# Single slices and an earlier spread in the first modulation, and scaled values made ahead of the delta rule's solves

## The chip, the cores and the metric

The kernel runs on one core of a Trainium2 chip. The metric is the device time of one execution in microseconds (us). The work is done by TensorE (matrix products, PE in the profile, its weight loads PEld), VectorE (DVE), ScalarE (ACT) and GpSimd (POOL). SyncE (SP) issues the loads and stores.

## What is computed

One block of a streaming encoder over 512 tokens of width 1024: a feed-forward half step, a token mixer of two head groups (gated delta rule and latent attention), and a second half step. Each of the three begins with an RMS norm that is modulated by a scale and a shift, which a product of the vector `silu(c)` with a large matrix gives.

```python
sc = jax.nn.silu(c)
mod = sc @ w_ada[l] + b_ada[l]
sh1, s1, g1, sh2, s2, g2, sh3, s3, g3 = jnp.split(mod, N_MOD, axis=-1)
h = _modulate(x, sh1, s1)              # rms(x) * (1 + s1) + sh1
x = x + 0.5 * g1 * _swiglu(h, ffn1_w_in[l], ffn1_w_out[l])
...
h = _modulate(x, sh2, s2)
x = x + g2 * _hybrid_mixer(h, ...)
```

The delta rule works in chunks. In each chunk a unit lower triangular system is solved:

```python
M = A + jnp.eye(CHUNK)
rhs = concatenate([v * beta, k * (beta * exp(G))], axis=-1)
W = triangular_solve(M, rhs)
u, wk = W[..., :GDN_DV], W[..., GDN_DV:]
```

`u` and `wk` then enter a recurrence over the chunks that carries the state.

## The kernel before

Tokens lie along the free dimension, features on the 128 partitions: `xT` is eight tiles of 128 x 512. Every weight and every activation that enters a large product is split into a high part (a copy by ScalarE to fp32r) and a low part (a subtraction by VectorE), and a product is three matmuls: high by high, high by low, low by high (`mm3`, L453 to L455).

A framework turns the program into queues. It places each instruction on its engine by the order of the program and by times that it estimates, gives each tile a buffer of its pool, and puts in the waits. Within `in_order()` every engine keeps the written order. Outside, instructions may move ahead of each other where their inputs allow it. Engines issue strictly in their final order. PSUM has eight banks: three in the pool `psa` (`acc()`, tiles pa) and five in `psb` (`aux()`, tiles pb). The pool `slots` holds 56 tiles of 128 x 512 floats.

**The first modulation** is `phase0`, written inside `in_order()`. It makes the transposed input, the first shift and scale, the modulated input `h` and at the same time the first three column groups of the feed-forward input product, six accumulators `pu`. The loop over `kt` walks the eight row blocks of the contraction. For each it needs a slice of `w_ada` (1024 rows by twice 128 columns, 1024 KB), a slab of 768 columns of `ffn1_w_in` (384 KB), and `h[kt]`.

A slice comes in one of two ways. `phase0_slice` loads one alone with two loads into a buffer of the pool `p0`, which has two buffers. `phase0_pair` loads two neighbours with eight loads into eight slots. Slices 0 and 1 are single, 2 and 3, 4 and 5, 6 and 7 are pairs. `phase0_weights(kt)` loads a slab into one of four buffers `wr`; the slab of step kt + 2 is asked for in step kt. The loads are on SyncE's queue in the written order.

From a slice come two columns, shift and scale. For slices 0 to 4 and 6 `phase0_cols` does it with sixteen small matmuls (L632), ScalarE copies the sums (L635), and `columns` adds four partial rows with matmuls (L525) and the bias with two VectorE instructions (L526, L527). Slices 5 and 7 (`SUMMED`) are instead summed up by `phase0_sum`, one ScalarE step (L641) and seven VectorE steps (L643) each, spread over the steps 2 to 5 of the loop by the table `STEPS`.

`raw(b, j)` transposes half of a token block with four TensorE transposes (L507) and copies the result to `xT` by VectorE (L508). There are eight such tiles: seven stand ahead of the first columns, the eighth behind them. The norm's factors `r` are computed per token. For block 0 the tokens are scaled (`xn`) before they are transposed (L547). VectorE copies this to SBUF (L549), ScalarE makes the high part with scale and shift (L552), VectorE the whole value (L553) and the low part (L554), and then the low weights (L556). Then come the six first products (L569). Behind them a product of ones with a diagonal matrix spreads `r` over all partitions (`spread_diag`, L663), and ScalarE copies it to `rb` (L571). All later blocks use `rb` in `modulated` (L688, L690, L677).

**The mixer** runs its dense units, 128 output columns each, on TensorE in program order, and steps side chains between them. `Rates` gives each chain so many steps for each step of the dense unit. `chain` carries the decay, the inverses of the blocks (`base_blocks`, `inverse`) and then the solves. `deltas` carries `delta_qk` and `delta_q`. `att` carries the attention. The units come in the order keys, queries, values, gates. In the gate units the rates are 1, 0.75 and 2.67.

`solve(p)` turns the values of block p to token-major order with four transposes (L1489, from `token_major`), scales them by VectorE into `vb` (L1269, from `mul`, line of a helper), scales the keys into `kbg` and `kd` in the same way, then multiplies with the inverse `U`: L1689 for `uu`, L1698 for `w`. `recur(p)` is the recurrence. The output products of the attention half (`out_attended`, update of `xT` at L2119) are stepped in as filling work, and the first weights of the last feed-forward part are split on the side (L1264, L1265).

Of the kernel before, what the change touches and what calls it, by code (L numbers as in the profile page):

```python
# [28 lines left out]
KPARTS = ((0, 8), (8, 8), (16, 6))  # L29
SEVEN = range(8, 21), range(4, 21)  # L30
SUMMED = (5, 7)
STEPS = {2: (5, range(4)), 3: (5, range(4, 8)), 4: (7, range(4)), 5: (7, range(4, 8))}


def drain(*gens):

    gens = list(gens)
    while gens:
        for g in list(gens):
            if next(g, "end") == "end":  # L40
                gens.remove(g)
# [51 lines left out]
class Block:  # L93
# [390 lines left out]
    def phase0(self):  # L484

        nc = self.nc
        xall = self.const([P, KT, NT], s="xT")
        self.xT = [xall[:, t, :] for t in range(KT)]
        v = self.small(NB, "v")
        slices, parts = [], []  # L490
        for kt in range(2):
            slices.append(self.phase0_slice(kt))
            parts.append(self.phase0_weights(kt))
        slices += self.phase0_pair(2)
        pv = self.aux()
        nc.tensor.transpose(pv[:, :80], self.vecs[:80, :], self.ident[:80, :80])
        self.sc = self.const([P, 8], s="sc")
        nc.scalar.activation(self.sc, pv[:, 72:80], AF.Silu)
        self.vT = self.const([P, 72], s="vT")
        nc.vector.tensor_copy(self.vT, pv[:, :72])  # L500
# [3 lines left out]
        def raw(b, j):  # L504
            pt = self.aux()
            for t in range(4):
                nc.tensor.transpose(pt[:, t * P:(t + 1) * P], self.xtok[b][:, (4 * j + t) * P:(4 * j + t + 1) * P], self.ident)  # L507
            nc.vector.tensor_copy(xall[:, 4 * j:4 * j + 4, b * P:(b + 1) * P], pt.rearrange("p (t c) -> p t c", t=4))  # L508

        tiles = [(b, j) for b in range(NB) for j in range(2)]  # L510
# [8 lines left out]
        self.c1, self.c2 = self.const([P, KT], s="sh"), self.const([P, KT], s="s1")  # L519
        self.new_h()  # L520

        def columns(kt, sg, pg, ones):
            k = slice(kt, kt + 1)
            for m in range(2):
                nc.tensor.matmul(pg[:, 256 + m:257 + m], sg[:, m * P:m * P + P], ones, start=True, stop=True)  # L525
            nc.vector.tensor_tensor(out=self.c1[:, k], in0=pg[:, 256:257], in1=self.vT[:, k], op=ALU.add)  # L526
            nc.vector.scalar_tensor_tensor(out=self.c2[:, k], in0=pg[:, 257:258], scalar=1.0, in1=self.vT[:, 8 + kt:9 + kt],  # L527
                                           op0=ALU.add, op1=ALU.add)

        def weights(kt):  # L530
            raw, hi, lo = parts[kt]
            self.split_w(raw[:, :6, :], hi[:, :6, :], lo[:, :6, :])
            return hi, lo
# [8 lines left out]
        raw0, wh, wl = (x[:, :6, :] for x in parts[0])  # L542
        w = wh, wl
        nc.scalar.copy(wh, raw0)
# [4 lines left out]
        nc.vector.tensor_copy(t, pt)  # L549
        columns(0, *cols)  # L550
        hh, hl = self.h[0]
        nc.scalar.activation(hh, t, AF.Identity, scale=self.c2[:, 0:1], bias=self.c1[:, 0:1])  # L552
        nc.vector.tensor_scalar(out=m, in0=t, scalar1=self.c2[:, 0:1], scalar2=self.c1[:, 0:1], op0=ALU.mult, op1=ALU.add)  # L553
        nc.vector.tensor_tensor(out=hl, in0=m, in1=hh.bitcast(F32), op=ALU.subtract)  # L554
        self.kept[0] = m, None
        nc.vector.tensor_tensor(out=wl, in0=raw0, in1=wh.bitcast(F32), op=ALU.subtract)  # L556
        raw(*tiles[7])
        pu = [self.acc() for _ in range(3)] + [self.aux() for _ in range(3)]
        sums = {}
        for kt in range(KT):  # L560
            (hi, lo), (xh, xl) = w, self.h[kt]
            more = kt + 1 < KT
            if kt + 2 < KT:
                parts.append(self.phase0_weights(kt + 2))
            if kt in (1, 3):
                slices += self.phase0_pair(kt + 3)
            if kt == 0:
                for j in range(6):
                    nc.tensor.matmul(pu[j], hi[:, j, :], xh, start=True, stop=False)  # L569
                rb = self.slot(s="rb")  # L570
                nc.scalar.copy(rb, self.spread_diag(dg, NB))  # L571
            for j in range(6):
                if j == 0 and more:
                    if kt > 2:
# [5 lines left out]
                    if kt in (1, 2):  # L580
                        w = weights(kt + 1)
                if j == (2 if kt + 1 in SUMMED else 1) and more:
                    columns(kt + 1, *cols)
                    made = self.modulated([kt + 1], slice(0, NT), rb, self.c2, self.c1, True)
                    next(made)
                    n, kcs = STEPS.get(kt, (None, ()))
                    for i, kc in enumerate(kcs):
                        if kt == 2 or i == 2:
                            drain(made)
                        if kc == 0:  # L590
                            sums[n] = self.slot(s="sg")[:, :256]
                        self.phase0_sum(sums[n], slices[n], kc)
                    drain(made)
                    if kt == 0:
                        w = weights(kt + 1)
                if kt > 0:
                    self.mm3(pu[j], hi[:, j, :], lo[:, j, :], xh, xl, False, kt == KT - 1)
                else:
                    nc.tensor.matmul(pu[j], hi[:, j, :], xl, start=False, stop=False)
                    nc.tensor.matmul(pu[j], lo[:, j, :], xh, start=False, stop=False)  # L600
        return pu
# [797 lines left out]
    def gates(self):  # L1399
# [9 lines left out]
        v.tensor_tensor(out=t4(x), in0=kv[:, :, 64:68], in1=self.dtb.unsqueeze(1).to_broadcast([P, NB, 4]), op=ALU.add)  # L1409
# [260 lines left out]
    def solve(self, p, vT):  # L1670
# [297 lines left out]
    def mixer(self, norms):  # L1968
# [21 lines left out]
                self.table(t, t, AF.Silu, after=after)  # L1990

        self.inv = [None] * NB
        self.kd, self.us, self.o, self.wk = ([None] * NB for _ in range(4))
        self.S = None

        def prepared():
# [208 lines left out]
```

## Time and profile before

| | us |
|---|---|
| median of 3 runs | 1041.88 (1041.50 to 1042.18) |
| the profiled execution | 1041.97 |
| its span | 1040.3 |

The span runs from the first to the last instruction that the profiler saw; the execution's time has 1.67 us more around it. In the lists of the profile a row is: start, duration, engine, line, operation, output and inputs with their shapes, count, and in brackets the idle time of the engine ahead of it with what ended it. Matmuls are pipelined, so the rows of TensorE overlap. The granted clock of TensorE was 1.000 over the whole span.

### The profile page before, as it was taken

To read this page: it belongs to the slowest core of one execution; us is meant where nothing else is said; L and a number is where in the kernel's file an instruction comes from. 1 tells how busy PE (TensorE), PEld (TensorE's weight loads), DVE (VectorE), ACT (ScalarE), POOL (GpSimd) and SP (SyncE) were. 2 spreads that over 40 slices of the span, in tenths; PEclk is the share of its full clock that TensorE was granted. 3 is DMA by queue.
4 is the path that set the end of the run, shared out by engine and by line. 5 is a ranking of instruction groups with operands and counts; after the bars stand their busy time and mean duration, and the time that the engine had idled before them with its cause. 6 is when DMAs were issued, how large, how long until landed. Compare 5 with 4: busy or idle time off the path is not lost.

```text
span 1040.3 us, 16767 instructions
## 1 busy us (share of the span) xinstructions
PE 1023.9 (98%) x6601; PEld 907.6 (87%) x6601; DVE 753.8 (72%) x1327; ACT 498.5 (48%) x910; POOL 29.6 (3%) x74
## 2 busy tenths in 40 slices
PE   7999999999999999999999989999999999999998
PEld 5788899999887898888788779998999999987888
DVE  5789788887787757868697467787788888783221
ACT  4452455556322235478864454364555555632221
POOL 0000000001000000000000001100000000000000
PEclk9999999999999999999999999999999999999999
DMA  9977234334688744211232031103333334383311
GB/s 330 320 230 255 76 89 122 89 116 130 213 297 280 241 126 130 61 42 41 61 83 65 21 87 36 42 24 96 105 92 112 108 97 121 114 271 105 112 48 42
DMA packets 201501, 130.77 MB, mean 126 GB/s; under 512 B 14017, under 2 KB 186062, under 8 KB 201422
## 3 DMA queue, kind: packets, MB, share of 16 engines
q1 hardware_dynamic: 201422, 129.69, 40.7%
q8 instruction: 52, 0.85, 0.3%
q14 instruction: 27, 0.22, 0.1%
HBM read 127.18 MB, written 2.49 MB: 125 GB/s over the span
## 4 chain that ended last, share of the span: by engine, by line
PE 93%; DVE 3%; issue 1%; DMA 1%; POOL 0%; SPq 0%; ACT 0%; POOLq 0%
PE pa L453 17%; PE pa L454 17%; PE pa L455 17%; PE pa L341 17%; PE pb L341 12%; PE pb L1937 1%; PE pb L453 1%; PE pb L455 1%; PE pb L454 1%; PE pb L1917 1%; DMA ar<-in_w_ada 1%; PE pb L1537 1%; PE pb L632 1%; PE pb L1919 0%; PE pb L1489 0%
## 5 line engine op out<-in xcount | busy, mean ns | idle before, releaser
L223 ACT CAST wh<-wr 128x1024 fp32r<-128x1024 f32 (+1 forms) x104 | 103.6, 1002 | 198.7 <-PE pa L454 174.8
L224 DVE TENSOR_TENSOR wl<-wr,wh 128x1024 fp32r<-128x1024 f32 (+1 forms) x104 | 120.5, 1163 | 80.6 <-ACT wh L223 78.6
L453 PE MATMUL pa<-ah,wh 128*128 128x512 f32 (+1 forms) x396 | 146.5, 370 | 0.0
L454 PE MATMUL pa<-al,wh 128*128 128x512 f32 (+1 forms) x396 | 145.0, 366 | 0.0
L455 PE MATMUL pa<-ah,wl 128*128 128x512 f32 (+1 forms) x396 | 144.9, 366 | 0.0
L257 DVE TENSOR_TENSOR wl<-wr,wh 128x1024 fp32r<-128x1024 f32 x90 | 110.0, 1223 | 44.4 <-ACT wh L261 44.4
L453 PE MATMUL pa<-hh,wh 128*128 128x512 f32 (+1 forms) x357 | 136.9, 384 | 0.0
L454 PE MATMUL pa<-hl,wh 128*128 128x512 f32 (+1 forms) x357 | 135.2, 379 | 0.0
L455 PE MATMUL pa<-hh,wl 128*128 128x512 f32 (+1 forms) x357 | 135.2, 379 | 0.0
L261 ACT CAST wh<-wr 128x1024 fp32r<-128x1024 f32 x90 | 91.8, 1052 | 2.7 <-DMA ar<-in_w_ada 1.8
L453 PEld LDWEIGHTS pa<-ah,wh 128*128 128x128 f32 x396 | 74.7, 189 | 14.5 <-ACT wh L223 2.5
L455 PEld LDWEIGHTS pa<-ah,wl 128*128 128x128 f32 x396 | 74.7, 189 | 12.1
L454 PEld LDWEIGHTS pa<-al,wh 128*128 128x128 f32 x396 | 74.7, 189 | 11.7
L453 PEld LDWEIGHTS pa<-hh,wh 128*128 128x128 f32 x357 | 67.3, 189 | 13.3 <-ACT th L1264 0.8
L813 DVE SCALAR_TENSOR_TENSOR aa<-ar,sc,aa 128x512 f32<-128x512 f32 x98 | 73.3, 749 | 6.3 <-DMA ar<-in_w_ada 4.3
L455 PEld LDWEIGHTS pa<-hh,wl 128*128 128x128 f32 x357 | 67.3, 188 | 11.6
L454 PEld LDWEIGHTS pa<-hl,wh 128*128 128x128 f32 x357 | 67.4, 189 | 10.7
L341 PE MATMUL pa<-hh,wh 128*128 128x256 f32 x240 | 68.0, 283 | 0.0
L341 PE MATMUL pa<-th,wh 128*128 128x256 f32 x240 | 67.9, 283 | 0.0
L341 PE MATMUL pa<-tl,wh 128*128 128x256 f32 x240 | 67.9, 283 | 0.0
L341 PE MATMUL pa<-th,wl 128*128 128x256 f32 x240 | 67.9, 283 | 0.0
L341 PE MATMUL pa<-hl,wh 128*128 128x256 f32 x240 | 67.9, 283 | 0.0
(434 smaller groups left out, 2375.3 us busy)
## 6 DMA issues: line engine op xcount, KB each, us to landing
wr<-in_ffn_w_in SPq DMA_DIRECT2D x79, 512.0 KB, 5.0
ar<-in_w_ada SPq DMA_DIRECT2D x104, 256.0 KB, 5.6
wr<-in_ffn_w_out SPq DMA_DIRECT2D x32, 512.0 KB, 4.2
wr<-in_w_in SPq DMA_DIRECT2D x21, 512.0 KB, 4.3
ar<-in_w_ada SPq DMA_DIRECT2D x20, 512.0 KB, 5.9
wr<-in_ffn_w_out SPq DMA_DIRECT2D x16, 384.0 KB, 4.7
wr<-in_w_out SPq DMA_DIRECT2D x8, 512.0 KB, 3.3
wr<-in_ffn_w_in SPq DMA_DIRECT2D x8, 384.0 KB, 5.9
```

The lines of the kernel that those rows point to most:

```text
L223: self.nc.scalar.copy(hi, raw)
L224: self.nc.vector.tensor_tensor(out=lo, in0=raw, in1=hi.bitcast(F32), op=ALU.subtract)
L257: sub = lambda out, x, y: nc.vector.tensor_tensor(out=out, in0=x, in1=y, op=ALU.subtract)
L261: nc.scalar.copy(hi[:, :n], raw[:, :n])
L341: nc.tensor.matmul(z, a[:, j, :], b, start=start and j == 0 and i == 0, stop=j == 3 and i == 2, skip_group_check=not start)
L453: mm(out, wh, xh, start=start, stop=False)
L454: mm(out, wh, xl, start=False, stop=False)
L455: mm(out, wl, xh, start=False, stop=stop)
L632: nc.tensor.matmul(pg[32 * q:32 * q + 32, :256], self.sc[:, kc:kc + 1].to_broadcast([P, 32]), a[kc], start=(e == 0), stop=(e == 1), tile_p ...
L813: nc.vector.scalar_tensor_tensor(out=acc, in0=a, scalar=sc, in1=acc, op0=ALU.mult, op1=ALU.add)
L1537: nc.tensor.matmul(pa[:, ps], kh[:, ps], x[:, ps], start=True, stop=True)
L1917: nc.tensor.matmul(ps[:, :n], self.qnT[h][:, ts], self.knT[h][:, :n], start=True, stop=False)
```

## The change

It has four parts.

First, the slices 0 to 3 are loaded singly. The pool `p0` has three buffers. The slabs 0 to 3 are asked for together with them, later ones three steps ahead.

Second, the order at the start of `phase0`. All eight tiles are transposed ahead of the first columns; ScalarE copies the last three. The spread stands ahead of the first products and `rb` right behind the low weights. The copy of the transposes of block 0 to SBUF goes away: ScalarE and VectorE read them from PSUM. The bias of shift and scale is put in one tile beforehand, and one VectorE instruction makes both columns.

Third, within the loop the split of the weights is separated into its two halves, `columns` always comes after the first group of products, and the steps of the two sums are dealt out by the table `ORDER` at three places of a step. In the mixer the copy of the decay constants is held behind the first instruction that needs the product of the units.

Fourth, a side chain `ahead` in `deltas` makes the four `vb`, with their transposes, during the gate units. `solve` makes one only if it isn't there.

```diff
-STEPS = {2: (5, range(4)), 3: (5, range(4, 8)), 4: (7, range(4)), 5: (7, range(4, 8))}
+ORDER = {2: ((), (), ((5, range(3)),)), 3: (((5, range(3, 5)),), ((5, range(5, 6)),), ((5, range(6, 8)),)),
+         4: ((), (), ((7, range(3)),)), 5: (((7, range(3, 5)),), ((7, range(5, 6)),), ((7, range(6, 8)),))}
...
-        for kt in range(2):
+        for kt in range(4):
             slices.append(self.phase0_slice(kt))
             parts.append(self.phase0_weights(kt))
-        slices += self.phase0_pair(2)
...
+        bias, c12 = (self.const([P, KT, 2], s=n) for n in ("cb", "c12"))
+        nc.vector.tensor_copy(bias[:, :, 0], self.vT[:, :8])
+        nc.vector.tensor_scalar(out=bias[:, :, 1], in0=self.vT[:, 8:16], scalar1=1.0, scalar2=None, op0=ALU.add)
+        self.c1, self.c2 = c12[:, :, 0], c12[:, :, 1]
...
+        def raw(i, copy):
+            b, j = divmod(i, 2)
+            pt = turned(self.xtok[b][:, j * NT:(j + 1) * NT])
+            copy(xall[:, 4 * j:4 * j + 4, b * P:(b + 1) * P], pt.rearrange("p (t c) -> p t c", t=4))
...
-        for i in range(4):
-            raw(*tiles[i])
+        for i in range(5):
+            raw(i, nc.vector.tensor_copy)
         r = self.rms_cols(v, NB, D)
-        for i in (4, 5, 6):
-            raw(*tiles[i])
+        for i in range(5, 8):
+            raw(i, nc.scalar.copy)
...
-            nc.vector.tensor_tensor(out=self.c1[:, k], in0=pg[:, 256:257], in1=self.vT[:, k], op=ALU.add)
-            nc.vector.scalar_tensor_tensor(out=self.c2[:, k], in0=pg[:, 257:258], scalar=1.0, in1=self.vT[:, 8 + kt:9 + kt],
-                                           op0=ALU.add, op1=ALU.add)
+            nc.vector.tensor_tensor(out=c12[:, kt, :], in0=pg[:, 256:258], in1=bias[:, kt, :], op=ALU.add)
...
-        t, m = self.slot(s="hm"), self.slot(s="hm")
-        nc.vector.tensor_copy(t, pt)
         columns(0, *cols)
+        pr = self.spread_diag(dg, NB)
         hh, hl = self.h[0]
-        nc.scalar.activation(hh, t, AF.Identity, scale=self.c2[:, 0:1], bias=self.c1[:, 0:1])
-        nc.vector.tensor_scalar(out=m, in0=t, scalar1=self.c2[:, 0:1], scalar2=self.c1[:, 0:1], op0=ALU.mult, op1=ALU.add)
+        m = self.slot(s="hm")
+        nc.scalar.activation(hh, pt, AF.Identity, scale=self.c2[:, 0:1], bias=self.c1[:, 0:1])
+        nc.vector.tensor_scalar(out=m, in0=pt, scalar1=self.c2[:, 0:1], scalar2=self.c1[:, 0:1], op0=ALU.mult, op1=ALU.add)
         nc.vector.tensor_tensor(out=hl, in0=m, in1=hh.bitcast(F32), op=ALU.subtract)
-        nc.vector.tensor_tensor(out=wl, in0=raw0, in1=wh.bitcast(F32), op=ALU.subtract)
-        raw(*tiles[7])
+        low(0)
+        rb = self.slot(s="rb")
+        nc.scalar.copy(rb, pr)
...
-            if kt + 2 < KT:
-                parts.append(self.phase0_weights(kt + 2))
+            if 3 < kt + 3 < KT:
+                parts.append(self.phase0_weights(kt + 3))
...
             for j in range(6):
                 if j == 0 and more:
...
+                    if kt > 2:
+                        if kt + 1 in SUMMED:
+                            high(kt + 1)
+                        low(kt + 1)
+                    for e in early[0]:
+                        steps(*e)
-                if j == (2 if kt + 1 in SUMMED else 1) and more:
+                if j == 1 and more:
                     columns(kt + 1, *cols)
                     made = self.modulated([kt + 1], slice(0, NT), rb, self.c2, self.c1, True)
                     next(made)
...
+                    for e in early[1]:
+                        steps(*e)
                     drain(made)
-                    if kt == 0:
-                        w = weights(kt + 1)
+                    if kt < 3:
+                        high(kt + 1)
+                        low(kt + 1)
+                    for e in early[2]:
+                        steps(*e)
...
-        with self.tc.tile_pool(name="p0", bufs=2) as self.p0:
+        with self.tc.tile_pool(name="p0", bufs=3) as self.p0:
...
-        v.tensor_copy(ea, self.alog)
+        self.follow(v.tensor_copy(ea, self.alog).ins, first.ins.name)
...
-        vb = self.slot(s="vb")
-        self.mul(h4(vb), h4(self.token_major(vT, p)), self.bc(self.kn[:, c4], 4))
-        kt = self.kt[p]
+        if self.vb[p] is None:
+            self.values(p, vT)
+        vb, kt = self.vb[p], self.kt[p]
...
+    def values(self, p, vT):
+        h4 = lambda x: x.rearrange("p (h d) -> p h d", h=4)
+        self.vb[p] = self.slot(s="vb")
+        self.mul(h4(self.vb[p]), h4(self.token_major(vT, p)), self.bc(self.kn[:, 4 * p:4 * p + 4], 4))
...
         chain.add(solving())
+
+        def ahead():
+            for p in range(4):
+                self.values(p, vT)
+                yield
+
+        deltas.add(ahead())
```

More of the change, by code (lines that the diff above doesn't have):

```diff
@@ L513, in phase0, with high, low @@
             nc.scalar.activation(jk, self.xtok[b], AF.Square, accum_out=v[:, b:b + 1])
-        for i in range(4):
-            raw(*tiles[i])
+        for i in range(5):
+            raw(i, nc.vector.tensor_copy)
         r = self.rms_cols(v, NB, D)
-        for i in (4, 5, 6):
-            raw(*tiles[i])
-        self.c1, self.c2 = self.const([P, KT], s="sh"), self.const([P, KT], s="s1")
+        for i in range(5, 8):
+            raw(i, nc.scalar.copy)
         self.new_h()
         def columns(kt, sg, pg, ones):
-            k = slice(kt, kt + 1)
             for m in range(2):
                 nc.tensor.matmul(pg[:, 256 + m:257 + m], sg[:, m * P:m * P + P], ones, start=True, stop=True)
-            nc.vector.tensor_tensor(out=self.c1[:, k], in0=pg[:, 256:257], in1=self.vT[:, k], op=ALU.add)
-            nc.vector.scalar_tensor_tensor(out=self.c2[:, k], in0=pg[:, 257:258], scalar=1.0, in1=self.vT[:, 8 + kt:9 + kt],
-                                           op0=ALU.add, op1=ALU.add)
[L530 to L533, printed above, removed]
+            nc.vector.tensor_tensor(out=c12[:, kt, :], in0=pg[:, 256:258], in1=bias[:, kt, :], op=ALU.add)
+        def high(kt):
+            raw, hi, _ = parts[kt]
+            nc.scalar.copy(hi[:, :6, :], raw[:, :6, :])
+        def low(kt):
+            raw, hi, lo = (x[:, :6, :] for x in parts[kt])
+            nc.vector.tensor_tensor(out=lo, in0=raw, in1=hi.bitcast(F32), op=ALU.subtract)
         xn = self.slot(s="xn")
@@ L541, in phase0 @@
         cols = self.phase0_cols(0, slices[0])
-        raw0, wh, wl = (x[:, :6, :] for x in parts[0])
-        w = wh, wl
-        nc.scalar.copy(wh, raw0)
+        high(0)
         pt = self.aux()
@@ L569, in phase0 @@
                     nc.tensor.matmul(pu[j], hi[:, j, :], xh, start=True, stop=False)
-                rb = self.slot(s="rb")
-                nc.scalar.copy(rb, self.spread_diag(dg, NB))
+            early = ORDER.get(kt, ((), (), ()))
             for j in range(6):
                 if j == 0 and more:
-                    if kt > 2:
-                        w = weights(kt + 1)
                     if kt + 1 in SUMMED:
@@ L585, in phase0 @@
                     next(made)
[L586 to L592, printed above, removed]
-                    drain(made)
-                    if kt == 0:
-                        w = weights(kt + 1)
+                    for e in early[1]:
+                        steps(*e)
+                    drain(made)
+                    if kt < 3:
+                        high(kt + 1)
+                        low(kt + 1)
+                    for e in early[2]:
+                        steps(*e)
                 if kt > 0:
@@ L1992, in mixer @@
         self.inv = [None] * NB
-        self.kd, self.us, self.o, self.wk = ([None] * NB for _ in range(4))
+        self.kd, self.us, self.o, self.wk, self.vb = ([None] * NB for _ in range(5))
         self.S = None
```

20 lines of the change are left out of this document (12 added, 8 removed).

## The prediction

> **What bounds the kernel now.** I read the profile page first, then busy time by 20 us stretches, then the timelines of the two places that the change touches: the start, and the solves of the delta rule after 600 us.
>
> ```profile
> PE 1023.9 (98%) x6601; PEld 907.6 (87%) x6601; DVE 753.8 (72%) x1327; ACT 498.5 (48%) x910; POOL 29.6 (3%) x74
> ...
> PE 93%; DVE 3%; issue 1%; DMA 1%; POOL 0%; SPq 0%; ACT 0%; POOLq 0%
> ...
> ar<-in_w_ada SPq DMA_DIRECT2D x104, 256.0 KB, 5.6
> wr<-in_ffn_w_out SPq DMA_DIRECT2D x32, 512.0 KB, 4.2
> ...
> wr<-in_ffn_w_in SPq DMA_DIRECT2D x8, 384.0 KB, 5.9
> ```
>
> ```profile
> 0.00:20.00 20.00, 13.03 (x85) 9.90 (x85) 10.12 (x25) 9.14 (x16) 2.35 (x12) 1.00 0.93 314
> 20.00:40.00 20.00, 20.00 (x128) 14.62 (x129) 13.02 (x27) 9.40 (x15) 0.00 (x0) 1.00 1.08 385
> ...
> 580.00:600.00 20.00, 20.00 (x170) 14.25 (x169) 9.00 (x24) 9.25 (x22) 0.00 (x0) 1.00 0.14 42
> 600.00:620.00 20.00, 17.23 (x141) 13.91 (x139) 13.05 (x28) 10.91 (x21) 2.02 (x2) 1.00 0.31 92
> ```
>
> After the span, the columns are busy time of TensorE, weight loads, VectorE, ScalarE and GpSimd, then clock, DMA share and GB/s. TensorE carries 93% of the chain that ended last and is full nearly everywhere, so the end moves only by TensorE work or by its idle time. Both places have idle time: 7.0 us in the first 20 us, 2.8 us between 600 and 620. From 20 us on TensorE is full, so a microsecond won at the start is kept.
>
> **The first modulation.** The timeline of the start:
>
> ```profile
> 3.61 0.23 DVE L500 COPY vT<-pb 128x72 f32<-128x72 f32 x1 [3.61 <-ACT sc L498]
> ...
> 12.33 1.09 PE L632 MATMUL pb<-ar,sc 128*32 128x256 f32 x16 [1.16 <-DMA ar<-in_w_ada]
> ...
> 14.05 0.69 DVE L549 COPY hm<-pb 128x512 f32<-128x512 f32 x1
> ...
> 14.66 0.15 DVE L526 TENSOR_TENSOR sh<-pb,vT 128x1 f32<-128x1 f32 x1
> 14.72 0.15 DVE L527 SCALAR_TENSOR_TENSOR s<-pb,vT 128x1 f32<-128x1 f32 x1
> 14.91 0.81 ACT L552 ACTIVATE hh<-hm,sh,s 128x512 fp32r<-128x512 f32 x1 [0.30 <-DVE s L527]
> ...
> 15.76 0.69 DVE L554 TENSOR_TENSOR hl<-hm,hh 128x512 fp32r<-128x512 f32 x1 [0.30 <-ACT hh L552]
> ...
> 15.77 0.97 PE L569 MATMUL pa<-hh,wh 128*128 128x512 f32 x3 [0.75 <-ACT hh L552]
> ...
> 16.36 0.95 DVE L556 TENSOR_TENSOR wl<-wr,wh 128x768 fp32r<-128x768 f32 x1
> ...
> 17.27 1.02 PE L663 MATMUL pb<-dg,ones 128*128 128x512 f32 x2
> 18.22 0.61 PEld L632 LDWEIGHTS pb<-ar,sc 128*32 128x32 f32 x16 [0.76 <-DVE xT L508]
> ...
> 19.24 0.50 PE L599 MATMUL pa<-hl,wh 128*128 128x512 f32 x1
> ...
> 22.80 1.09 PE L632 MATMUL pb<-ar,sc 128*32 128x256 f32 x16
> ...
> 28.65 1.09 PE L632 MATMUL pb<-ar,sc 128*32 128x256 f32 x16
> ```
>
> The first columns of the modulation (L632 at 12.33) wait for their slice from memory; the change leaves this alone. Behind them come the copy of the transposes (L549), two VectorE steps to the columns, the high part (L552) and the six first products. After those stand the spread (L663, 1.02 us) and then, held by the copy of the eighth transposed tile (L508), the second columns at 18.22.
>
> The change takes L549 out and makes one VectorE step of the two. L527 began 0.06 us after its twin L526, so the high part can begin at about 14.8 instead of 14.91. It then reads PSUM; a row of that kind stands below (L1964, 0.69 us against L552's 0.81). The first product then comes at about 15.55, a gain of 0.2 (bounds 0 and 0.3).
>
> The spread goes ahead of the first products, where TensorE stood idle for 0.75 us. The eighth tile goes ahead of the columns, where it waited 1.16 us for the slice. Its copy goes to ScalarE with two others (about 0.7 us each by L549), which is busy for only 9.14 of the first 20 us. So the second columns follow the six products directly: 15.55 plus the 1.50 from 15.77 to 17.27 is 17.05, against 18.22, a gain of 1.17. The products at 19.24 come at about 18.1. Their low operand must be there: the steps at 14.91 (L553), 15.76 and 16.36 now follow each other from a PSUM source.
>
> Two engines read the bank of these transposes, ScalarE for the high part and VectorE for the whole value. At 3.61 VectorE's copy of another bank, which needs nothing of ScalarE's result there, is released by ScalarE's read of it. I take the same wait here: VectorE begins at 15.55, and with 0.61 us from L549 to its follower L526, 0.60 (L554 to L556) and 0.95 the low weights are there at 17.7. They are first needed by the product behind the one at 18.1, which the row at 19.24 lets begin within 0.5 us; I take 18.4. So the wait costs nothing, but 0.7 us are left where without the wait it would be about 1.2. The Trainium skill, "PSUM — Partial Sum Buffer", section "PSUM bank collisions raise a hardware error", says that two engines must not access one bank at once, two reads included, and that compilers add a dependency; by that rule the wait comes, as in the row at 3.61.
>
> Does the memory keep pace? The loads by window:
>
> ```profile
> DMA packets 6673, 6.28 MB, mean 314 GB/s; under 512 B 248, under 2 KB 6161, under 8 KB 6673
> ...
> DMA packets 5140, 5.37 MB, mean 384 GB/s; under 512 B 300, under 2 KB 5139, under 8 KB 5139
> ```
>
> The first row is 0 to 20 us, the second 16 to 30. Before, the queue holds x (4 times 512 KB), two single slices (1024 KB each, two loads of 512), two weight slabs (384 KB each) and the pair of slices 2 and 3 (8 times 256 KB): 7.1 MB. With 6.28 by 20 us and 384 GB/s after, the pair is in at 22.2; its columns run at 22.80. Were they to come 1.2 us sooner with the pair kept, they would wait about 0.6. With singles, slice 2 needs only 6.1 MB and is in by 19.5; slice 3, behind a third slab, by 23.2, where its columns ran at 28.65. On SyncE's queue slice 3 now waits for the buffer of slice 0, free when its columns end at 13.4, and slab 4 for that of slab 0, free at 17.7; the loads ahead of them keep the queue longer than that, so those behind lose nothing. Eight fewer slots are taken here. So the loads take nothing of the gain.
>
> In the later steps the sums of slices 5 and 7 are dealt out otherwise. VectorE is nearly full there:
>
> ```profile
> 35.00:40.00 5.00, 5.00 (x34) 3.75 (x27) 4.61 (x11) 2.19 (x4) 0.00 (x0) 1.00 1.08 380
> ```
>
> ```profile
> 39.46 1.00 DVE L643 SCALAR_TENSOR_TENSOR sg<-ar,sc,sg 128x256 f32<-128x256 f32 x2
> ```
>
> The sixth columns now come after one group of three products instead of two, and the fourth step has five sums on VectorE instead of four (0.5 us each by the second row). I take 0.2 us of waiting there, bounds 0 and 0.6. The sum of this half: -1.17 + 0.2 = **-1.0 us** (bounds -1.4 and -0.4).
>
> The copy of the decay constants (L1412, 0.16 us on VectorE near 50 us, TensorE full over it) is put at its place in the mixer: nothing.
>
> **The delta rule.** The first row is the view of the tile of the gates (its four units end from 567.9 to 600.4), the others are the timeline of the stage after 600 us:
>
> ```profile
> L1980 ACT COPY z<-pa x4: 575/588/591, 567.9 to 600.4; 128x512 f32<-128x512 f32 x4
> ```
>
> ```profile
> 609.19 0.42 DVE L1665 TENSOR_SCALAR U<-pb 64x256 f32<-64x256 f32 x1
> ...
> 610.92 0.50 PE L454 MATMUL pa<-ml,wh 128*128 128x512 f32 x1 [0.34 <-DVE ml L1965]
> ...
> 612.89 0.63 PE L1959 MATMUL pb<-ident,on 128*128 128x128 f32 x4 [0.77 <-DVE on L1269]
> ...
> 613.55 0.69 ACT L1964 ACTIVATE mh<-pb,cwT 128x512 fp32r<-128x512 f32 x1 [4.36 <-PE pb L1959]
> ...
> 614.16 0.42 DVE L1665 TENSOR_SCALAR U<-pb 64x256 f32<-64x256 f32 x1 [1.09 <-PE pb L1663]
> ...
> 614.67 0.71 PE L1489 MATMUL pb<-ident,cv 128*128 128x128 f32 x5
> ...
> 616.12 1.41 DVE L2119 SCALAR_TENSOR_TENSOR xT<-pa,mod,xT 128x512 f32<-128x512 f32 x2 [0.88 <-PE pa L455]
> ...
> 617.44 0.68 DVE L1265 TENSOR_TENSOR fl<-fr,fh 128x512 fp32r<-128x512 f32 x1
> 618.04 0.68 DVE L1269 TENSOR_TENSOR vb<-pb,kn 128x512 f32<-128x512 f32 x1
> ...
> 618.87 2.33 PE L1689 MATMUL pb<-vb,U 128*128 128x128 f32 x16 [1.66 <-DVE vb L1269]
> ...
> 622.91 1.16 PE L1689 MATMUL pb<-vb,U 128*128 128x128 f32 x8 [0.38 <-DVE vb L1269]
> ```
>
> The inverses are done by 614.6 and the value transposes (L1489) by 615.4, but the scaled values (vb) stand on VectorE behind two updates that wait for TensorE, and behind a split. TensorE waits 1.66 us for the first and 0.38 us for the third: 2.04 in all. Four transposes take 0.44 on the chain:
>
> ```profile
> 624.07 0.44 PE pb L1489 x4
> ```
>
> The change makes transposes and products in the second side chain. By its rate of 0.75 it has twelve steps during the sixteen of the gate units. By my count of the yields three of them finish older work, so the four values take the fourth to seventh: the second and third unit, some 570 to 585 us. TensorE is full there: 4 x 0.44 = 1.8 us are added. The same 1.8 us leave the solves. VectorE is idle for half of 580 to 600, which covers four products of 0.68. In the solves TensorE work is then 1.8 shorter and the 2.04 idle have lost their cause. What is late next is the scaled keys (same size, same queue): without four vb, 2.7 us lighter, they come early enough. Net **-2.0 us**. Bounds: 0, if the keys take the values' place, and -3.1, if the ready products also fill the 0.34 and 0.77.
>
> Sum: -1.0 - 2.0 = -3.0. The profiled execution took 1041.97 us (span 1040.3 and 1.67 around it), 0.09 above the median of the runs, 1041.88. So I forecast 1038.9.
>
> **Rivals.** (a) The solves give back only what the gate units pay: the keys and the updates on VectorE become the wait. For it: VectorE is busy without a gap from 616.12 on. Against it: 2.7 us of that are the values. Then -1.0: 1040.9.
> (b) The free products also fill the other gaps: -1.0 - 3.1, so 1037.8. For it: U of the first block was ready at 609.6, and the row at 614.67 shows that work is drawn forward.
> (c) The start gains nothing, since the bank's wait holds the low weights beyond 18.4; it decides only if VectorE is 0.7 us later than worked out. Then 1039.9.
> (d) Slower: each group of transposes in the gate units holds one of five small PSUM banks until VectorE has read it, while attention and the inverses share them with TensorE full. If TensorE stands for each group's 0.68 us, and rival (a) holds too, that is -1.0 + 1.8 + 2.7 = +3.5: 1045.4. It decides once the products wait on VectorE. Against it: VectorE is half idle there.
> (e) That the values aren't made ahead at all would need the side chain to run dry; the count above leaves five steps over. It then equals (a).
>
> **The numbers.** A measurement of this kernel tells about 0.2% (2.1 us) from no change: faster is below 1039.8, slower above 1044.0. Chances: forecast 0.50 (1037.9 to 1040.1, four fifths of it below 1039.8), (a) with (e) 0.20, (b) 0.14, (c) 0.05, (d) 0.11. Faster: 0.40 + 0.14 + half of (c) and a little of (a), 0.58. Slower 0.11, the same 0.31. The range takes in the forecast, (b), (c) and most of (a), 1036.9 to 1041.9, and leaves out (d) and the edges.
>
> **What would show it.** Right: the second columns near 17.05 right behind six first products, L663 ahead of them, the columns of slice 2 near 21.7 with no DMA wait, phase 0 some 1.0 us shorter; value transposes between 565 and 585, no idle on vb before L1689, the recurrence some 2 us nearer to its place in the start-shifted trace. Wrong: TensorE idle ahead of the products at 18.1, or ahead of the columns for slices 2 to 5; new idle time in 565 to 600 with VectorE as releaser; L1698 waiting for the keys.

## The result and the profile after

| | before | after |
|---|---|---|
| median of 21 runs each, us | 1042.71 (1041.45 to 1044.98) | 1041.12 (1040.62 to 1042.23) |
| ratio, 95% interval | | 0.9986 (0.998 to 0.9992) |
| the profiled execution, us | 1041.97 | 1040.80 |
| its span, us | 1040.3 | 1039.1 |

The change gains 1.6 us by the medians, half of the 3.0 that were forecast. In the profiled executions, where the span is 1.2 us shorter, the two halves went opposite ways: the first modulation lost 1.2 us, where a gain of 1.0 was worked out, and the delta rule gained 1.8, where 2.0 was. The rest is a shift of 0.4 us between the two places, told below, and 0.2 behind them. The ratios here and below leave out one execution that fell in a slower state, 1113 us in the run e_align.

**The start.** The timeline of the changed kernel; L646 are the columns (L632 before), L556 the high part, L557 the whole value, L582 the six first products:

```profile
13.01 1.09 PE L646 MATMUL pb<-ar,sc 128*32 128x256 f32 x16 [2.12 <-DMA ar<-in_w_ada]
...
15.07 1.10 PE L677 MATMUL pb<-dg,ones 128*128 128x512 f32 x2
...
15.50 0.78 ACT L556 ACTIVATE hh<-pb,c 128x512 fp32r<-128x512 f32 x1 [0.22 <-DVE c L532]
...
16.31 0.81 DVE L557 TENSOR_SCALAR hm<-pb,c 128x512 f32<-128x512 f32 x1 [0.85 <-ACT hh L556]
16.33 0.97 PE L582 MATMUL pa<-hh,wh 128*128 128x512 f32 x3 [0.15 <-ACT hh L556]
...
17.76 0.95 DVE L540 TENSOR_TENSOR wl<-wr,wh 128x768 fp32r<-128x768 f32 x1
...
17.92 1.09 PE L646 MATMUL pb<-ar,sc 128*32 128x256 f32 x16
...
18.94 0.50 PE L613 MATMUL pa<-hl,wh 128*128 128x512 f32 x1
...
22.51 1.09 PE L646 MATMUL pb<-ar,sc 128*32 128x256 f32 x16
...
28.32 1.09 PE L646 MATMUL pb<-ar,sc 128*32 128x256 f32 x16
...
34.14 2.65 PE L646 MATMUL pb<-ar,sc 128*32 128x256 f32 x16
36.72 0.50 PE L454 MATMUL pa<-hh,wh 128*128 128x512 f32 x1
...
46.09 1.09 PE L646 MATMUL pb<-ar,sc 128*32 128x256 f32 x16
```

The kernel before had these columns for slices 4 and 6:

```profile
34.47 1.09 PE L632 MATMUL pb<-ar,sc 128*32 128x256 f32 x16
```

```profile
44.90 1.09 PE L632 MATMUL pb<-ar,sc 128*32 128x256 f32 x16
```

From the first columns to the second it is now 17.92 - 13.01 = 4.91 us, against 18.22 - 12.33 = 5.89 before: the new order does its work. But the first columns come 0.68 later, and the sixteen small products for slice 4 take 2.65 us in place of 1.09: they begin when the first quarters of the pair are in and then stand for 1.56 us. The chain of waits names the reason; its rows are start, duration and what the chain ran through. First the kernel before, where the chain leaves the loads with slice 0 and runs on compute engines from then on:

```profile
4.00 8.20 DMA ar<-in_w_ada
12.33 1.14 PE pb L632 x16
```

The changed kernel, where it goes through a slab and a piece of the pair of slices 4 and 5 until 36.1:

```profile
23.12 7.00 DMA wr<-in_ffn_w_in
30.13 6.00 DMA ar<-in_w_ada
36.17 0.62 PE pb L646 x2
```

The loads themselves, by windows (0 to 20, 20 to 40; the columns are those of the table of windows in the prediction):

```profile
0.00:20.00 20.00, 12.65 (x87) 9.42 (x88) 8.24 (x22) 10.49 (x19) 2.35 (x12) 1.00 0.96 285
20.00:40.00 20.00, 19.74 (x120) 13.80 (x120) 11.85 (x21) 8.83 (x15) 0.00 (x0) 1.00 1.11 340
```

The share of the DMA engines (0.96 and 1.11) is at least what it was (0.93 and 1.08), yet they move 285 and 340 GB/s, where it was 314 and 385. The queue isn't idle: it is slower.

**The delta rule.** The gate units' tile, the scaled values and the value transposes by tile and line, then the solves in the timeline (L1679 is L1665 before, L1703 L1689, L1712 L1698):

```profile
L1999 ACT COPY z<-pa x4: 572/589/591, 568.7 to 603.1; 128x512 f32<-128x512 f32 x4
...
L1283 DVE TENSOR_TENSOR vb<-pb,kn x4: 652/665/684, 572.1 to 583.6; 128x512 f32<-128x512 f32 x4
...
L1503 PE MATMUL pb<-ident,cv x48: 270/272/329, 471.1 to 580.0; 128*128 128x128 f32 x48
```

```profile
616.78 0.71 PE L1703 MATMUL pb<-vb,U 128*128 128x128 f32 x4
...
621.60 1.13 PE L1712 MATMUL pb<-U,kbg 128*128 128x128 f32 x8 [0.68 <-DVE kbg L1283]
...
628.14 0.59 ACT L1759 COPY o<-pb 128x512 f32<-128x512 f32 x1 [0.36 <-PE pb L1757]
```

All four values are made from 572 to 584 us. No product waits for them any more; the one new wait is 0.68 us for the first scaled keys. The same place of the recurrence in the trace before:

```profile
629.17 0.59 ACT L1740 COPY o<-pb 128x512 f32<-128x512 f32 x1 [0.94 <-PE pb L1738]
```

The gate units began 0.8 us late (568.7 against 567.9), ended 2.7 late and the recurrence is 1.0 early. So the gates pay 1.9 us and the solves give back 3.7: a gain of 1.8 from the first gate unit on.

### The profile page after: what moved, and what is told of

The parts are those of the page before. It is cut to its first block, busy times and chain, and to the rows that moved or that the text cites. A ratio compares the mean times of both kernels' runs of the same rounds, so it can differ in the third digit from the quotient of the medians.

```text
span 1039.1 us, 16767 instructions
## 1 busy us (share of the span) xinstructions
PE 1023.8 (99%) x6601; PEld 907.3 (87%) x6601; DVE 750.8 (72%) x1317; ACT 499.7 (48%) x913; POOL 29.7 (3%) x74
## 4 chain that ended last, share of the span: by engine, by line
PE 93%; DMA 2%; DVE 2%; issue 1%; SPq 1%; POOL 0%; ACT 0%; POOLq 0%
PE pa L454 17%; PE pa L455 17%; PE pa L456 17%; PE pa L342 17%; PE pb L342 12%; DMA ar<-in_w_ada 1%; PE pb L1956 1%; PE pb L1936 1%; PE pb L1551 1%; PE pb L454 1%; PE pb L456 1%; PE pb L455 1%; DMA wr<-in_ffn_w_in 1%; SPq L132 1%; PE pb L1503 1%
## 5 line engine op out<-in xcount | busy, mean ns | idle before, releaser
L224 ACT CAST wh<-wr 128x1024 fp32r<-128x1024 f32 (+1 forms) x97 | 97.8, 1015 | 197.3 <-PE pa L455 179.1
L225 DVE TENSOR_TENSOR wl<-wr,wh 128x1024 fp32r<-128x1024 f32 (+1 forms) x97 | 113.8, 1178 | 75.6 <-ACT wh L224 73.9
```

The costliest lines, as they stand in the source:

```text
L224: self.nc.scalar.copy(hi, raw)
L225: self.nc.vector.tensor_tensor(out=lo, in0=raw, in1=hi.bitcast(F32), op=ALU.subtract)
```

## The experiments

In the profile the DMA records have a duration for each packet. I took the mean over all packets of one size that start in one window: 512 bytes from 9.5 to 14 us (some 2,000 packets) and 1024 bytes from 28 to 36 us (some 2,000). Here are all runs with these means, the start of the columns of slices 0, 4 and 6, the time by which one of the columns took longer than 1.09 us, and the ratio to the kernel before, measured side by side with it. "Moved" is by how many bytes the buffers of the weights and slices stand off their place in the kernel before.

| kernel | moved | 512 / 1024 B, ns | slice 0 | 4 | 6 | stands | ratio (95%) |
|---|---|---|---|---|---|---|---|
| before | 0 | 27 / 46 | 12.33 | 34.47 | 44.90 | 0 | 1 |
| after | 64 | 32 / 51 | 13.01 | 34.14 | 46.09 | 1.56, slice 4 | 0.9986 (0.998 to 0.9992) |
| r_after | 64 | 31 / 51 | 13.73 | 36.14 | 46.57 | 0 (0.87 by the clock, slice 0) | 0.9981 (0.9972 to 0.999) |
| e_first | 64 | 32 / 51 | 13.28 | 34.34 | 45.99 | 1.29, slice 4 | 1.0001 (0.9993 to 1.001) |
| e_values | 0 | 27 / 46 | 12.18 | 34.27 | 44.69 | 0 | 0.9982 (0.9973 to 0.9991) |
| e_pair | 64 | 31 / 51 | 13.16 | 35.89 | 46.31 | 1.67, slice 2 | 0.9997 (0.9988 to 1.0006) |
| e_align | 0 | 27 / 46 | 12.83 | 33.91 | 44.34 | 0 | 0.997 (0.9958 to 0.9982) |
| e_shift64 | 64 | 32 / 51 | 12.90 | 36.34 | 46.76 | 0.74, slice 2 | 1.0027 (1.0018 to 1.0036) |
| e_shift256 | 256 | 27 / 46 | 12.26 | 34.39 | 44.81 | 0 | 1.0004 (0.9994 to 1.0013) |
| e_best | 0 | 27 / 46 | 12.27 | 33.34 | 43.77 | 0 | 0.9966 (0.9953 to 0.9978) |
| e_start | 0 | 27 / 46 | 12.79 | 33.86 | 44.28 | 0 | 0.9989 (0.9979 to 0.9998) |
| e_shift128 | 128 | 32 / 51 | 13.04 | 35.81 | 46.26 | 0.75, slice 2 | 1.0018 (1.0009 to 1.0027) |
| e_slab | 64 | 32 / 51 | 12.94 | 34.03 | 45.24 | 0.82, slice 4 | 0.998 (0.9971 to 0.9989) |

**Which half, and is it the loads' order?** Four runs. r_after is the change once more.

> The changed kernel once more. Its profiled execution had packets of 512 bytes at 32 ns between 9.5 and 28 us where the one before had 27, and TensorE waited 1.56 us at the columns of slice 4. Theory L (the loads set the pace of the first modulation, by the queue's order and the length of its runs): the wait at those columns is there again, 1 to 2 us, whatever the packets take, and the kernel is again 1 to 2 us faster than the one before. Theory M (that execution's memory was slow by chance): packets at 27 ns again, no wait at those columns, the kernel near 3 us faster. Theory V (the bank's wait and the new order on VectorE cost the gain): no wait for a load, TensorE waits for VectorE ahead of products.

The ratio is as good, and the packets are as slow, which theory M does not allow. The wait at the columns of slice 4, which theory L has, isn't there. In this execution the granted clock was 0.5 from 13.6 to 17.0 us, so the columns of slice 0 took 1.96 us and those of slice 1 began at 19.95, 6.22 us after them instead of 4.91:

```profile
13.73 1.96 PE L646 MATMUL pb<-ar,sc 128*32 128x256 f32 x16 [2.30 <-DMA ar<-in_w_ada]
```

With the slice itself 0.7 us later, everything was 2 us later from there on, and the pair came in time. That the packets are slow is no chance; whether a wait shows depends on how far TensorE has come.

e_first is the change without the values ahead:

```diff
-        deltas.add(ahead())
```

> The change without the values made ahead: its first three parts alone. Theory L: slower than before by 0.5 to 1.3 us, with TensorE waiting for the slices of the pair 4 and 5, and the second columns still earlier than before. Theory M: 1.0 us faster in a fast execution. Theory V: slower with no wait for loads.

No gain against the kernel before: the time lies between the numbers of the theories. Of the 1.4 us that the profiled execution's span is longer, 1.0 is a lower clock in the solves, told at the end. The wait for the loads is the one that theory L has, at the same place:

```profile
34.34 2.38 PE L646 MATMUL pb<-ar,sc 128*32 128x256 f32 x16
```

e_values is the kernel before with the fourth part alone (`values` and `ahead`, and `solve` taking what is there).

> The kernel before with the values made ahead and nothing else. All theories: the solves return their 2 us, so 1.8 to 2.3 us faster than before, no TensorE idle time with vb as releaser. If instead the gain in the solves comes only from the shift of the start, it is below 1 us.

A gain of 1.9 us by the ratio, and 1.8 by the trace from the first gate unit on: its gates begin 0.3 us early and its recurrence is 2.1 us early, for the two rows below stand against 567.9 and 629.17. The second half of the change does what was worked out, alone and with the first.

```profile
L1985 ACT COPY z<-pa x4: 575/588/592, 567.6 to 602.0; 128x512 f32<-128x512 f32 x4
```

```profile
627.04 0.59 ACT L1745 COPY o<-pb 128x512 f32<-128x512 f32 x1 [0.36 <-PE pb L1743]
```

e_pair is the change with the old loads for slices 2 and 3: a pair in eight pieces behind slab 1, and slabs 2 and 3 behind it.

```diff
-        for kt in range(4):
+        for kt in range(2):
             slices.append(self.phase0_slice(kt))
             parts.append(self.phase0_weights(kt))
+        slices += self.phase0_pair(2)
+        parts += [self.phase0_weights(kt) for kt in (2, 3)]
```

> The whole change, but with slices 2 and 3 loaded as a pair again, in runs of 1024 bytes, right behind slab 1. Theory L: 2.1 MB take about 6 us of the 16 engines at 46 ns for 1024 bytes against 7 to 8 at 27 to 32 ns for 512, so pair 4 and 5 comes 1 to 2 us sooner and the wait at the columns of slice 4 falls to under 0.6 us; the columns of slice 2 wait instead, 0.3 to 1.2 us. Altogether 0.3 to 1 us faster than the change. Theories M and V: nothing is won at the columns of slice 4, those of slice 2 wait, so 0.5 us slower than the change.

Here the theory that order and run length of the loads are the whole cause fell. Slice 4 came without standing, as it says, but 1.75 us later than in the change, since slice 2 became the one that stands, for 1.67 us where at most 1.2 were expected, and by the ratios the kernel is 1.1 to 1.7 us slower than the change, where theory L has it faster.

```profile
22.63 2.76 PE L648 MATMUL pb<-ar,sc 128*32 128x256 f32 x16
```

And its 1024-byte packets still took 51 ns, where the same pieces took 46 before. What the four runs with slow packets have in common is not an order but a place. The constants `cb` and `c12` take 64 bytes each per partition, `sh` and `s1`, which they replace, took 32 each. So the pool of constants is 64 bytes larger and every pool behind it moves: the first buffer of the slabs begins at byte 56384 of its partition, before at 56320, a multiple of 256.

**The place of the target.** e_align is the change with the bias in a slot instead of a constant, which puts all buffers back:

```diff
-        bias, c12 = (self.const([P, KT, 2], s=n) for n in ("cb", "c12"))
+        bias = self.slot(s="cb")[:, :2 * KT].rearrange("p (k m) -> p k m", m=2)
+        c12 = self.const([P, KT, 2], s="c12")
```

> The whole change, but the bias of shift and scale lies in a slot and not in a constant of its own. In the change the constants grow by 64 bytes per partition, and with them every weight buffer, slot and slice buffer begins 64 bytes further on: at 56384 instead of 56320 for the first slab, no longer a multiple of 256. Theory A (the place of the load's target: each packet takes some 5 ns more when its target is shifted by 64 bytes): packets of 512, 1024 and 1536 bytes are back at 27, 46 and 65 ns between 10 and 40 us as before, the pair of slices 4 and 5 comes in time, the first modulation wins its 1.0 us, and the kernel is about 3 us faster than before, 1.5 us faster than the change. Theory L (the order of the queue and the run length alone): packets stay at 32, 51 and 70, and the time at the change's.

e_shift64 is the kernel before with a constant of 64 bytes that nothing reads, e_shift256 the same with 256 bytes (`[P, 64]`):

```diff
+        nc.gpsimd.memset(self.const([P, 16], s="pad"), 0.0)
```

> The kernel before with one constant of 64 bytes per partition more, which nothing reads, so that every buffer behind the constants is shifted by 64 bytes. Theory A: packets of 512, 1024 and 1536 bytes take 32, 51 and 71 ns between 10 and 40 us, the pair of slices 2 and 3 is late by about 1.5 to 2 us, and the kernel is 1 to 2 us slower than before. Theory L: packets and time as before.

> The kernel before with a constant of 256 bytes more, which nothing reads. Theory A with a step of 256 bytes: packets at 27, 46 and 65 ns, the time as before. If a step of 512 bytes is what counts: packets slower as with 64. Theory L: as before.

All three came out as the place of the target says. The windows from 20 to 40 us, e_align, then e_shift64, then e_shift256:

```profile
20.00:40.00 20.00, 20.00 (x126) 14.70 (x126) 13.28 (x24) 9.39 (x15) 0.00 (x0) 1.00 1.07 365
```

```profile
20.00:40.00 20.00, 19.59 (x121) 13.51 (x122) 11.23 (x23) 8.43 (x15) 0.00 (x0) 1.00 1.09 354
```

```profile
20.00:40.00 20.00, 20.00 (x128) 14.64 (x128) 13.11 (x27) 9.39 (x15) 0.00 (x0) 1.00 1.08 384
```

With one fill more than the kernel before, which e_shift256 has too, 64 bytes of offset take the memory from 385 to 354 GB/s, let TensorE stand in a stretch that was full (0.74 us at slice 2; the way from the columns of slice 3 to those of slice 4 takes another 0.62 more than before), and make the kernel before 0.27% (2.8 us) slower; 256 bytes change nothing that can be measured. The 2.8 us are more than the 1 to 2 that were expected, and a part of them may be the clock: its mean over these executions is 0.998, beside 0.999 for the kernel before. The means of the executions with a clock of 1.000 differ by 1.8 us (1043.6 for four, against 1041.8 for nine of the kernel before). Taking the offset out of the change makes the columns of slice 4 run without standing, and the time is 0.3% (3.1 us) below before, where the forecast was 3.0:

```profile
33.91 1.09 PE L647 MATMUL pb<-ar,sc 128*32 128x256 f32 x16
```

e_best is e_align with slab 4 asked for behind the pair 4 and 5, the weights of step 4 split behind the columns of slice 4, and the fifth and seventh columns after two groups again.

> The whole change with the bias in a slot, and slab 4 asked for behind the pair of slices 4 and 5, its halves made behind the columns of slice 4; the columns of slices 5 and 7 again after two groups of products. Theory A: nothing waits for that pair any more once the packets are quick, so this is level with the run that only moves the bias, within 0.4 us. Theory L: the pair comes 1.1 us sooner than in the change, and this is about 1 us faster than the run that only moves the bias.

The best of all, 3.5 us below before by the ratio. But its profiled execution is ahead of e_align's by 0.56 us from slice 0 on (12.27 against 12.83), and from there to slice 6 both take the same 31.5 us. The intervals overlap: that the order of the slab is worth something, once the buffers stand right, isn't shown.

**What is left: the first half alone, the step of the offset, the order of the slab.** e_start is e_first with the edit of e_align.

> The first three parts of the change without the values made ahead, and with the bias constant in one of the slots, so that the loads' targets keep their place as in the kernel before. Theory (place of the load's target): packets of 1024 bytes take 46 ns again between 20 and 40 us, no columns wait for a pair, and the first modulation alone is worth what the change with the same edit gained less what the values gained alone, about -1.0 to -1.2 us, as the prediction's sum for this half: 1040.7 beside a median of 1041.8. Rival (the first half is worth nothing by itself, and its gain showed only beside the values): no change against the kernel before, like the run of the first three parts with the targets moved.

With the buffers in their place the first half gains by itself: 0.11% (1.1 us), where e_first gained nothing, and no columns stand. The rival, that this half is worth nothing, is out, if narrowly (the interval ends at 0.9998). The profiled execution shows the gain at the start (44.28 against 44.90 for slice 6, although slice 0 came 0.46 late) and loses part of it in the solves, where the granted clock fell to 0.93:

```profile
620.00:640.00 20.00, 20.00 (x140) 18.80 (x139) 14.69 (x25) 10.03 (x22) 3.06 (x3) 0.93 0.10 28
```

e_shift128 is e_shift64 with 128 bytes (`[P, 32]`).

> The kernel before with a constant of 128 bytes per partition that nothing reads. With 64 bytes the packets between 10 and 40 us grew from 27, 46 and 65 ns to 32, 51 and 71, with 256 bytes they did not. If what counts is that a target begins at a multiple of 256 bytes: packets as with 64 bytes, and about 2 to 3 us slower than before. If a multiple of 128 bytes is enough: packets and time as before, within 0.6 us. Between the two, if each packet pays for the number of smaller pieces it is cut into.

Packets as with 64 bytes, and slice 2 stands for 0.75 us as there. The kernel is 1.9 us slower by the ratio, and 1.6 by the means of the executions with a clock of 1.000 (1043.5 for three, against 1041.9 for fourteen).

```profile
23.47 1.84 PE L633 MATMUL pb<-ar,sc 128*32 128x256 f32 x16
```

So a multiple of 128 is not enough. The price in these windows is about 5 ns a packet of 512 bytes and 5 a packet of 1024, with 64 bytes as with 128: between these two sizes and these two offsets it goes with the packet, not with its bytes nor with how far it stands off.

e_slab is the change as it is, with slab 4 behind the pair as in e_best (and slab 6 behind the pair 6 and 7), and the split of the weights and the later columns set back as there (not shown):

```diff
-            if 3 < kt + 3 < KT:
-                parts.append(self.phase0_weights(kt + 3))
...
+            if 3 < kt + 3 < KT:
+                parts.append(self.phase0_weights(kt + 3))
```

> The change as it is, targets moved by 64 bytes, but with slab 4 asked for behind the pair of slices 4 and 5 instead of ahead of it, and the split of that slab and the place of the fifth columns set back accordingly. Theory (place of the target makes the loads late, and the pair 4 and 5 is where it shows): the columns of slice 4 come 1.0 to 1.5 us sooner, with no or little waiting, though packets still take 32 and 51 ns; the time falls to about 2.5 us below the kernel before, where the change was 1.6 to 2.0 below it. Rival (the lost time moves on): the next slab is late instead, and the time stays within 0.4 us of the change's distance.

Half of what was expected. Slice 4 stands for 0.82 us instead of 1.56, and slice 6 comes 0.85 sooner than in the change:

```profile
34.03 1.91 PE L649 MATMUL pb<-ar,sc 128*32 128x256 f32 x16
```

The time is 1.9 us below before by the medians, the change's was 1.6 below, with intervals that overlap. The trace has the theory's sign, but the time is where the rival put it, within 0.4 us of the change's; the times don't settle it.

## Why the prediction was right or wrong

**The failed step is the memory.** "So the loads take nothing of the gain" rested on 384 GB/s from 20 us on, taken over from the kernel before. The kernel after had these rates, from 16 to 30 us:

```profile
DMA packets 6260, 4.51 MB, mean 322 GB/s; under 512 B 174, under 2 KB 6259, under 8 KB 6259
```

A second error sits in the same number. With the buffers in place the loads of the change had 367 GB/s in that window in e_start, 369 in e_best and 335 in e_align, so 384 was too high for them even there: their single slices come in packets of 512 bytes, 27 ns or 19 bytes a ns, where a pair's 1024 bytes take 46 ns, 22 bytes a ns. By e_start and e_best, some 45 of the missing 62 GB/s belong to the place of the target. Why e_align's execution had less is open; its columns came in time all the same.

The prediction counted bytes, buffers and places in the queue, and the new constants only as one tile. It did not ask where the pools behind that tile come to stand. Its own list had the sign by which it would be wrong, and that sign came: TensorE idle ahead of the columns for slices 2 to 5. The Trainium skill, "DMA: Bandwidth & Descriptors", section "How a descriptor splits into AXI transactions", says that a descriptor is split at multiples of 256 bytes, and that where it does not start at one, its first transaction starts at the multiple below and fetches bytes that go unused. By that rule a packet of 512 or 1024 bytes that starts off such a multiple takes one transaction more. The measured steps agree with a price of that kind: 5 ns more for a packet, whether it is 512 or 1024 bytes and whether it stands 64 or 128 bytes off, and none at 256. But the page speaks of what is read, and here the written side stands off. That it is this cut is argued from the page; the runs show the price and the step.

**The sum of the first half, term by term.** Slice 0 came 0.68 us late. From slice 0 to slice 4 the change took 21.13 us against 22.14, a gain of 1.01. Slice 4 stood for 1.56, and the rest took 10.39 against 10.43. Together +1.19, which is what the kernel is late at slice 6. The forecast's gain of 1.0 is in it; the two losses are loads. Without the offset, slice 0 to slice 6 takes 31.5 us (e_align, e_best, e_start) against 32.57: 1.1 gained.

**What held in it.** The second columns follow six first products directly, and the spread stands ahead of them. The gain there was 0.98 instead of 1.17: the first product began 0.83 us after the high part did, for which 0.75 was taken, and the six products took 1.59 instead of 1.50. VectorE waited for ScalarE's read of the bank, as in the row at 3.61 (0.85, released by L556). It cost nothing: the products behind the second columns came 1.02 us after them, as before. That part of rival (c) fell with it. For the later steps 0.2 us of waiting were taken; without the slow loads there was none.

**The delta rule.** Forecast: 1.8 us paid in the gate units, 3.84 given back in the solves. Measured: 1.9 and 3.7. The values came in the stretch that the count of the side chain's steps gave (570 to 585, measured 572 to 584). TensorE stayed full there (20.00 us of 20 between 580 and 600), so rival (d) did not happen, and (a) only in a trace: 0.68 us of waiting for the first keys. Rival (b) is out too; more than 3.84 was not given back.

**A hit for the wrong reason.** 1041.12 lies within the range and near rival (a)'s 1040.9, but (a) put the loss into the solves. The loss was in the half whose working seemed the surer one, and no rival named slower loads. That the time fell into the range all the same is luck.

A shift of 0.4 us between 520 and 565 us (the change is 1.2 late ahead of it and 0.8 behind) was not foreseen. All runs show between 0.1 and 0.7 us of it, those without the first three parts too (0.5 in e_shift128, 0.3 in e_shift256, 0.2 in e_shift64 and e_values), so it need not come from the change. It may be that the profiled execution of the kernel before lost time there; no run takes it apart.

## What to carry to other kernels

A constant that grows by some bytes moves every buffer behind it. Where loads are the bound, as here between 10 and 40 us, see that their targets begin at multiples of 256 bytes, and when an edit makes an unrelated load late, compare the durations of single packets of one size before looking at the order of the queue. A forecast that takes a rate over from another kernel should say what the rate hangs on: size of the pieces and place of the target, not only bytes.

## What the runs showed of the hardware

- A target that stands 64 or 128 bytes off a multiple of 256 costs about 5 ns a packet between 10 and 40 us, where the queue is full: 27 to 32 for 512 bytes, 46 to 51 for 1024, and 65 to 71 for 1536 (28 to 36 us). For the kernel before that alone is 1.9 to 2.8 us by the ratios, and 1.6 to 1.8 by the executions with a clock of 1.000.
- Later it hardly shows, although the same buffers stand off and the DMA engines are as good as full: between 280 and 300 us (DMA share 0.98 and 0.99) packets of 512 bytes take 28 ns in the kernel before and after. So the place alone does not make the price. What else does is open.
- When slice 0 lands differs from one execution to the next: its columns began between 12.18 and 12.83 us with the buffers in place, between 12.90 and 13.73 with them off.
- In four of the profiled executions the granted clock was 0.5 for one stretch of 3.4 us: in r_after from 13.6 us, and in the solves in e_first (from 621.0), e_start (619.2) and e_shift256 (619.9), so that their means between 620 and 640 us are 0.91, 0.93 and 0.92, where it was 1.00 in the kernel before and after. In e_first the sixteen products of the first values then took 2.93 us, where they took 2.33 before:

```profile
619.45 2.93 PE L1703 MATMUL pb<-vb,U 128*128 128x128 f32 x16 [1.64 <-DVE vb L1283]
```

Over the solves each of the three loses 1.0 us against the kernel before: e_first is 0.6 us late ahead of them and 1.6 behind, e_start 1.3 early and 0.3, e_shift256 0.4 early and 0.6 late. All three lack the values made ahead, but so do the kernel before, e_shift64 and e_shift128, whose clock stayed at 1.00 there. And e_shift256 has the instructions of the kernel before and one fill, so the first half of the change isn't needed for the stretch. What decides it from one execution to the next no run shows.
